# Second products of two FFNs: six of 22 half-pairs by seven quarter products

## The chip, the cores and the metric

One core of one Trainium2 chip runs the whole program. The metric is the device time of one execution in microseconds (us), the median of several runs. The engines are named as in the profile: PE (TensorE, matmuls) with its weight loads PEld, DVE (VectorE), ACT (ScalarE), POOL (GpSimd) and SP (SyncE), whose queue issues the loads. Each engine works through its own instructions in order; they wait for each other by semaphores.

## The reference, cut to what matters

One decoder layer on 512 tokens of width 1024 in float32: an FFN, a token mixer, and a second FFN, each between norms and added to `x`.

```python
def swiglu_ffn(x, w_in, w_out):
    gate, up = jnp.split(x @ w_in, 2, axis=-1)
    return (jax.nn.silu(gate) * up) @ w_out
...
    x = x + 0.5 * rms_norm(swiglu_ffn(rms_norm(x, norm_pre[l, 0]), ffn1_w_in[l], ffn1_w_out[l]), norm_post[l, 0])
    mixed = token_mixer(rms_norm(x, norm_pre[l, 1]), ...)
    x = x + rms_norm(mixed, norm_post[l, 1])
    x = x + 0.5 * rms_norm(swiglu_ffn(rms_norm(x, norm_pre[l, 2]), ffn2_w_in[l], ffn2_w_out[l]), norm_post[l, 2])
```

`ffn1_w_out` and `ffn2_w_out` are 2816 x 1024. The change is in the products `(...) @ w_out`, called the second products here: 512 tokens, 2816 hidden channels, 1024 columns.

## The kernel before, in words

**Number format.** A float32 operand is split into two parts that the matmul takes: `hi`, a rounded copy made by ACT, and `lo`, the rest, made by DVE. A product is three matmuls, hi hi, hi lo and lo hi (`mm3`, lines 125 to 129). Making the two parts is called a conversion here: one ACT cast and one DVE subtraction, of 128 x 1024 elements for a weight tile (`split`, lines 209 and 211) as for a hidden tile (`h_tile`, lines 672 and 673).

**Weights.** `weights` (line 136) turns a list of items, in the order of use, into loads with due places. Loads go out on SP's queue into rings of raw buffers (`raw`, 3 deep, and `raw2`, 5 deep; the second products use `raw2`). `split` converts the next item into one of four slots of one large tile `w`; `feed` does so while fewer than four slots are taken, `pull` hands a slot to the matmuls, `drop` gives it back. A slot can begin 16 elements earlier (`late`).

**First products** (`ffn_in`, `prod`, `after`). They already use seven products instead of eight on quarter matrices; their matmuls have 256 columns (line 489). Their left operands lie in the four tiles `xq` and in three tiles with the tag `s`; POOL adds raw weights for them (line 223). Their result, the hidden rows `hf`, is 22 rows of 128 channels x 512 tokens.

**Second products** (`ffn_out`, line 676). Two adjacent rows of `hf` are a pair (`PAIRS` is 11). The 1024 output columns are taken in two halves of 512. For each half, for each of the 11 pairs, the kernel converts the pair's hidden tile (`h_tile`, three buffers with the tag `s`; the last one goes to `xq[3]`), pulls the weight tile of 2 x 128 rows by 512 columns, and runs, for each of four chunks of 128 tokens, 2 x 3 matmuls of 512 columns into that chunk's accumulator, a bank of PSUM. One pair in one half is a half-pair: 24 matmuls; there are 22 in each FFN. After the first half-pair the last first product (`p4` of the last group) is run. PSUM has eight banks, handed out by `ps`; the four accumulators of a half take four.

**The end of a stage.** The first half's accumulators are squared and multiplied by the norm's gain (`post0`). The last four half-pairs of the second half are held back: their four weights are pulled together, and then the chunks are finished one after the other (`mm`, called by `last`, line 406): chunk 0 with all four weights, then chunk 1, 2 and 3. After each chunk come the post-norm and the addition to `x` (`post1`), and, in the first FFN, the next norm (`norm`). The transposes of the normed rows on PE (`trans`) stand after chunk 2 for chunk 0 and inside chunk 3 for chunk 1. In the second FFN the rows are stored and there is nothing to transpose.

**What sets the order.** Here the order is not written out by hand (only the program's start is). The code is traced from top to bottom; a planner then lets each engine take, of what is ready at its place in a planned time line, what was traced first, and writes this order down for good. Buffers of one tag are handed out as they come free.

Of the kernel before, what the change touches and what calls it, by code (L numbers as in the profile page):

```python
# [14 lines left out]
P = 128  # L15
# [43 lines left out]
class Item:  # L59

    def __init__(self, key, loads, rows=None, adds=(), dst=None):
        self.key, self.loads, self.rows, self.adds, self.dst = key, loads, rows, adds, dst
        self.reads = {key, *(k for pair in adds for k in pair)}


class Layer:
# [117 lines left out]
    def split(self):  # L186
# [5 lines left out]
        if it.dst:  # L192
            w = it.dst()
        else:
            if self.wt is None:
                self.wt = self.wp.tile([P, 2 * D * WBUF + PAD], F32R, name="w")

            taken = {(n, late) for n, late, _ in self.slot.values()}
            fit = [(n, late) for late in (True, False) for n in self.free if (n - 1 if late else n + 1, not late) not in taken]
            n, late = next(f for f in fit if not f[1] or (it.key[0] == "mix" and b == 512))  # L200
# [453 lines left out]
    def ffn_in(self):  # L654
# [8 lines left out]
        self.feed()  # L663
        self.lag()

    def h_tile(self, k2, dst=None):

        t = dst
        if t is None:
            t = self.place(self.hpool.tile([P, 2 * D + PAD], F32R, tag="s", bufs=3, name=self.name("hs")), 2)  # L670
        src = self.hf[:, 2 * k2 : 2 * k2 + 2, :]
        self.nc.scalar.copy(t[:, 0], src)
        self.nc.vector.tensor_tensor(t[:, 1], src, t[:, 0].bitcast(F32), op=ALU.subtract)  # L673
        return t

    def ffn_out(self, gpost_row, scale, after, trans, head):
        NK2, LAST = PAIRS, 4
        seq = [k2 for _ in range(2) for k2 in range(NK2)]
        hs = self.hs
        made = [len(hs)]  # L680

        def more(n):
            while made[0] < min(n, len(seq)):
                k2 = seq[made[0]]
                last = made[0] == len(seq) - 1
                dst = self.xq[3].rearrange("p b k t -> p b (k t)").rearrange("p b (k t) -> p b k t", k=2) if last else None
                hs.append(self.h_tile(k2, dst))
                made[0] += 1

        def out_mm(ps, w, h, k2, i):  # L690
            for kk in range(2):
                k = 2 * k2 + kk
                s = slice(i * P, (i + 1) * P)
                self.mm3(ps, h[:, 0, kk, s], h[:, 1, kk, s], w[:, 0, kk, :], w[:, 1, kk, :], k == 0, k == NF - 1)

        g = self.gain("gpost", gpost_row)
        ys = []
        n = 0
        for half in range(2):
            acc = [self.ps() for _ in range(NT)]  # L700
            for k2 in range(NK2 - LAST if half else NK2):
                more(n + 2)
                w = self.pull()
                more(n + 3)
                h = hs.popleft()
                for i in range(NT):
                    out_mm(acc[i], w, h, k2, i)
# [9 lines left out]
        for k2 in range(NK2 - LAST, NK2):  # L717
# [12 lines left out]


# [73 lines left out]
    def ffn_items(self, name, w_in, w_out):  # L805
# [29 lines left out]
            dst = (lambda n=stay[p]: self.stay[n]) if p in stay else None  # L835
            made.append(Item((name, t, place[p]), own.get((p, t), ()), None, adds.get((p, t), ()), dst))
        for h in range(2):
            for k2 in range(PAIRS):
                src = w_out[k2 * 2 * P : (k2 + 1) * 2 * P, h * 512 : (h + 1) * 512].rearrange("(k p) d -> p k d", p=P)
                key = (name, "out", h, k2)  # L840
                made.append(Item(key, [Load(key, src, 2, 512, "raw2", 5, 8)]))
                if h == k2 == 0:
                    made.append(Item((name, PAIRS - 1, "a"), ()))
        return made

    def small_params(self):

# [711 lines left out]
```

## Time and profile before

| | us |
|---|---|
| median of 3 runs | 937.13 |
| lowest, highest | 936.61, 937.19 |
| profiled execution, device time | 936.74 |
| its span in the trace | 935.0 |
| PE busy | 926.7 |
| DVE busy | 700.1 |
| ACT busy | 468.7 |
| second products of the first FFN in the span, about | 226 to 350 |
| second products of the second FFN, about | 806 to 929 |

All durations in the prediction are from the profiled execution. Times in the trace count from the span's start. A group row shows line, engine, operation, output <- inputs, shapes and count, then busy time, the mean duration of one in ns, and the idle time of the engine before such instructions with what ended it. A row of the order in time begins with start and duration in us. A matmul's duration reaches past the start of the next one, so that what matmuls cost is read from their starts.

### The profile page before, as it was taken

What the parts mean: (1) busy time and instruction counts of PE and PEld (TensorE: products, weight loads), DVE (VectorE), ACT (ScalarE), POOL (GpSimd) and SP (SyncE); (2) the same over time, 40 slices, a digit from 0 to 9 for tenths busy, and PEclk for the clock granted to TensorE, in tenths of its full rate; (3) what the DMA queues carried; (4) which work ended last, traced back from release to release, by engine and by line L of the source; (5) the groups of instructions that cost most, each with busy time, mean ns of one, the idle gap of its engine ahead of it and who ended that gap; (6) DMA issues with size and microseconds to landing.
All of it is one profiled execution on the core that took longest, in us unless ns stands there. A gap on an engine that the chain in (4) does not pass through costs nothing.

```text
span 935.0 us, 16820 instructions
## 1 busy us (share of the span) xinstructions
PE 926.7 (99%) x7021; PEld 850.6 (91%) x7021; DVE 700.1 (75%) x785; ACT 468.7 (50%) x639; POOL 289.9 (31%) x225
## 2 busy tenths in 40 slices
PE   9999999999999999999999999999999999999997
PEld 7999999999888889998888888999999999988885
DVE  6798999998545466688766655887999999844543
ACT  7645445455334345987654254853444454534431
POOL 3535555661000027000020301445455655100001
PEclk9999999999999999999999999999999999999999
DMA  9243334425323005422423135213333422332202
GB/s 318 89 136 114 113 97 131 128 99 158 113 91 106 7 3 126 108 83 70 136 70 113 46 108 185 90 46 113 114 111 117 134 91 91 116 110 91 91 0 91
DMA packets 81992, 97.10 MB, mean 104 GB/s; under 512 B 4178, under 2 KB 61558, under 8 KB 81915
## 3 DMA queue, kind: packets, MB, share of 16 engines
q1 hardware_dynamic: 81306, 94.44, 32.4%
q8 instruction: 55, 0.90, 0.4%
q0 software_dynamic: 320, 1.06, 0.3%
q10 hardware_dynamic: 288, 0.52, 0.2%
q14 instruction: 23, 0.18, 0.1%
HBM read 93.90 MB, written 2.11 MB: 103 GB/s over the span
## 4 chain that ended last, share of the span: by engine, by line
PE 97%; DVE 1%; POOL 1%; issue 1%; ACT 1%; DVEq 0%; POOLq 0%; ACTq 0%
PE ps L489 46%; PE ps L127 13%; PE ps L129 13%; PE ps L128 13%; PE ps L434 6%; PE ps L268 1%; PE ps L1058 1%; POOL col L355 0%; PE ps L1328 0%; PE ps L1131 0%; PE ps L1296 0%; PE ps L116 0%; ACT junk L354 0%; PE ps L123 0%; PE ps L1097 0%
## 5 line engine op out<-in xcount | busy, mean ns | idle before, releaser
L211 DVE TENSOR_TENSOR w<-raw,w 128x1024 fp32r<-128x1024 f32 x214 | 364.2, 1710 | 129.5 <-ACT w L209 129.5
L209 ACT CAST w<-raw 128x1024 fp32r<-128x1024 f32 x214 | 223.9, 1052 | 305.6 <-PE ps L129 104.5
L223 POOL TENSOR_TENSOR raw<-raw,raw 128x1024 f32<-128x1024 f32 x80 | 221.0, 2763 | 171.8 <-DVE w L211 161.3
L489 PE MATMUL ps<-xq,w 128*128 128x256 f32 x2016 | 238.1, 277 | 0.0
L489 PEld LDWEIGHTS ps<-xq,w 128*128 128x128 f32 x2016 | 233.7, 188 | 0.2
L489 PE MATMUL ps<-sq,w 128*128 128x256 f32 x1440 | 171.0, 277 | 0.0
L489 PEld LDWEIGHTS ps<-sq,w 128*128 128x128 f32 x1440 | 167.4, 188 | 0.0
L129 PE MATMUL ps<-w,hs 128*128 128x512 f32 x336 | 131.0, 390 | 0.0
L127 PE MATMUL ps<-w,hs 128*128 128x512 f32 x336 | 130.9, 390 | 0.0
L128 PE MATMUL ps<-w,hs 128*128 128x512 f32 x336 | 130.8, 389 | 0.0
L127 PE MATMUL ps<-w,xq 128*128 128x512 f32 x208 | 83.2, 400 | 0.1
L128 PE MATMUL ps<-w,xq 128*128 128x512 f32 x208 | 81.0, 390 | 0.0
L129 PE MATMUL ps<-w,xq 128*128 128x512 f32 x208 | 81.0, 391 | 0.0
L129 PEld LDWEIGHTS ps<-w,hs 128*128 128x128 f32 x336 | 63.1, 188 | 13.8 <-DVE hs L673 0.7
L127 PEld LDWEIGHTS ps<-w,hs 128*128 128x128 f32 x336 | 63.1, 188 | 13.0
L128 PEld LDWEIGHTS ps<-w,hs 128*128 128x128 f32 x336 | 63.1, 188 | 12.8
L355 POOL TENSOR_SCALAR col<-col 128x1 f32<-128x1 f32 x24 | 10.5, 437 | 198.8 <-ACT junk L354 198.6
L434 PE MATMUL ps<-xq,w 128*128 128x256 f32 x480 | 55.8, 278 | 0.0
L434 PEld LDWEIGHTS ps<-xq,w 128*128 128x128 f32 x480 | 55.4, 188 | 0.2 <-issue 0.2
L673 DVE TENSOR_TENSOR hs<-hf,hs 128x1024 fp32r<-128x1024 f32 x42 | 51.1, 1217 | 0.0
L355 POOL TENSOR_SCALAR col<-col,col 128x1 f32<-128x1 f32 x24 | 10.0, 418 | 119.5 <-ACT junk L354 119.2
L129 PEld LDWEIGHTS ps<-w,xq 128*128 128x128 f32 x208 | 39.0, 188 | 8.8 <-DVE xq L275 0.3
(233 smaller groups left out, 939.5 us busy)
## 6 DMA issues: line engine op xcount, KB each, us to landing
raw<-in_ffn_w_in_dram SPq DMA_DIRECT2D x88, 512.0 KB, 4.4
raw<-in_ffn_w_out_dram SPq DMA_DIRECT2D x44, 512.0 KB, 3.9
raw<-in_w_mix_in_dram SPq DMA_DIRECT2D x28, 512.0 KB, 3.8
raw<-in_w_mix_out_dram SPq DMA_DIRECT2D x8, 512.0 KB, 3.7
out_dram<-xs SPq DMA_DIRECT2D x8, 256.0 KB, 2.1
xs<-in_x_dram SPq DMA_DIRECT2D x6, 256.0 KB, 6.2
gpost<-in_norm_post_dram SPq DMA_DIRECT2D x3, 512.0 KB
gpre<-in_norm_pre_dram SPq DMA_DIRECT2D x2, 512.0 KB, 4.1
```

The costliest lines, as they stand in the source:

```text
L127: mm(ps, sh, mh, start=start, stop=False, **kw)
L128: mm(ps, sh, ml, start=False, stop=False, **kw)
L129: mm(ps, sl, mh, start=False, stop=stop, **kw)
L209: nc.scalar.copy(hi, raw)
L211: nc.vector.tensor_tensor(lo, raw, hi.bitcast(F32), op=ALU.subtract)
L223: nc.gpsimd.tensor_tensor(o, o, c, op=ALU.add)
L268: self.nc.tensor.transpose(pt[:, c * P : (c + 1) * P], src[:, k * P : (k + 1) * P], self.ident)
L355: nc.gpsimd.tensor_scalar(m, ss, s2 / D, b, op0=ALU.mult, op1=ALU.add)
L434: mm(ps[:, u0:u1], w[:, a, k, :], self.xop(k, b, u0, u1), start=k + n + m == 0, stop=k == ND - 1 and n == 2, skip_group_check=True,)
L489: self.nc.tensor.matmul(ps[:, c], wb[b][:, k, v], left[d][:, k, :], start=first and a + n + k == 0, stop=n == 2 and k == KH - 1, skip_grou ...
L673: self.nc.vector.tensor_tensor(t[:, 1], src, t[:, 0].bitcast(F32), op=ALU.subtract)
L1058: nc.tensor.matmul(sc[r, o : o + u.stop - u.start], k8[:, m, r], q8[:, m, u], start=True, stop=True, skip_group_check=True)
```

## The change

Of the 11 pairs, three (3, 4 and 2) are computed in both halves by seven quarter products instead of eight: six of 22 half-pairs. For one such half-pair the hidden tile is a 2 x 2 matrix of quarters (two rows of `hf` by two halves of the tokens), and the weight tile is a 2 x 2 matrix too (two rows by two halves of the 512 columns). Products 1 to 7 each multiply a quarter or a sum of quarters, 128 channels by 256 tokens with 128 channels by 256 columns: two chunks of tokens, three matmuls of 256 columns each.

- **Order.** `OUT` lists both halves: `p` is a plain half-pair, `k` and `s` go by seven products, `r` is plain with a hidden tile that the first half left over. The four last half-pairs of the second half are plain.
- **Sums of weights.** After the first conversion of a weight tile of `k` or `s`, DVE forms four differences in place in the raw tile (`w_sums`, each 128 x 256); the raw tile is then converted a second time into another slot. So such a half-pair pulls two slots.
- **Sums of hidden quarters.** `s_tile` forms four sums (DVE, 128 x 256 each), in place in `hf` or, for pair 2 in the first half, in two extra tiles, and converts them. Pairs 3 and 4 keep both converted tiles in the four `xq` tiles for the second half; pairs 9 and 10, last in the first half, are first in the second, with the tiles still there.
- **Banks.** Products 2, 3 and 4 go straight into the accumulators. Products 1, 5, 6 and 7 go into four further banks, each with both chunks, and are summed there over the half's three such pairs.
- **Gather.** After the last of the three, one ACT copy and four DVE additions form four terms in SBUF, in `hf` rows no longer needed. One plain half-pair is run; then, ahead of each chunk's matmuls of the next plain half-pair, DVE adds that chunk's term to its accumulator.
- **Ends.** Chunks 0 and 1 run through the last four weights together: weight 0 for both, weight 1 for both, and so on.
- **Places.** `h_tile` begins 112 elements later in its buffer; weight slots of the second products may begin 32 elements earlier.

```diff
+OUT = ("p0 p1 p5 k3 k4 p6 s2 p7 p8 p10 p9".split(), "r9 r10 k3 k4 s2 p0 p1 p5 p6 p7 p8".split())
...
+            taken = {n: late for n, late, _ in self.slot.values()}
+            want = 0 if b != 512 else 1 if it.key[0] == "mix" else 2
+            fits = lambda n, late: taken.get(n - 1, 2) >= late >= taken.get(n + 1, 0)
+            n, late = next((n, late) for late in (*range(want, -1, -1), 1, 2) for n in self.free if fits(n, late))
...
+        if it.then:
+            it.then(raw)
...
+                if kind == "k" and h == 0:
+                    kept[k2] = self.h_tile(k2, homes.popleft()), self.s_tile(k2, homes.popleft())
+                elif kind == "s":
+                    kept[k2] = self.h_tile(k2), self.s_tile(k2, None, h == 0)
+                elif kind == "p":
+                    kept[k2] = self.h_tile(k2, flat(self.xq[3]) if made[0] == len(seq) - 1 else None), None
+                hs.append(kept[k2])
...
+        def seven(acc, sums, begun, w, wt, h, hs_, stop):
+            tok = lambda q, t: slice(HALF * q + P * t, HALF * q + P * (t + 1))
+            col = lambda q: slice(HALF * q, HALF * (q + 1))
+            for p, a, ka, qa, b, kb, qb in (
+                (1, h, 0, 0, w, 0, 0), (5, hs_, 1, 1, wt, 0, 0), (6, hs_, 0, 0, wt, 1, 1), (7, hs_, 0, 1, wt, 0, 1),
+                (2, h, 1, 0, w, 1, 0), (3, hs_, 1, 0, w, 1, 1), (4, h, 1, 1, wt, 1, 0),
+            ):
+                fresh = p in sums and p not in begun
+                begun.add(p)
+                for t in range(2):
+                    if p in sums:
+                        out = sums[p][:, col(t)]
+                    else:
+                        out = acc[2 * (p == 4) + t][:, col(p == 3)]
+                    for m, (x, y) in enumerate(((0, 0), (0, 1), (1, 0))):
+                        self.nc.tensor.matmul(
+                            out, a[:, x, ka, tok(qa, t)], b[:, y, kb, col(qb)],
+                            start=fresh and t + m == 0, stop=stop and m == 2, skip_group_check=True,
+                        )
+
+        def gather(sums, pairs):
+            x, y = (self.hf[:, 2 * k : 2 * k + 2, :].rearrange("p t (c v) -> p t c v", c=2) for k in pairs)
+            u = self.sp.tile([P, D], F32, tag="xn", bufs=1, name=self.name("u2"))[:, :512]
+            two = lambda t: t.rearrange("p (t v) -> p t v", t=2)
+            self.nc.scalar.copy(x[:, :, 0], two(sums[1]))
+            add(two(u), two(sums[6]), x[:, :, 0])
+            add(x[:, :, 1], two(sums[5]), two(u))
+            add(y[:, :, 0], two(sums[7]), two(u))
+            add(y[:, :, 1], two(sums[5]), y[:, :, 0])
+            return [t[:, i].rearrange("p c v -> p (c v)") for t in (x, y) for i in range(2)]
...
+                if kind in "pr":
+                    since += terms is not None
+                    for i in range(NT):
+                        if since == 2:
+                            add(acc[i], acc[i], terms[i])
+                        out_mm(acc[i], w, h, i, m == 0, since == 1 or m == PAIRS - 1)
+                else:
+                    seven(acc, sums, begun, w, wt, h, hs_, k2 == fast[-1])
+                    self.drop(wt)
                 self.drop(w)
+                if fast and k2 == fast[-1]:
+                    terms = gather(sums, [k for _, k, kind in self.outs(0) if kind == "k"])
...
-            for m, (k2, w) in enumerate(ws):
-                out_mm(acc[i], w, hs[m], k2, i)
+            for m, (k2, w) in enumerate(ws if i != 1 else ()):
+                for j in (0, 1) if i == 0 else (i,):
+                    out_mm(acc[j], w, hs[m][0], j, False, m == LAST - 1)
...
+                made.append(Item(key, [Load(key, src, 2, 512, "raw2", 5, 8)], then=self.w_sums if kind in "ks" else None))
+                if kind in "ks":
+                    made.append(Item(key, ()))
...
+    def w_sums(self, raw):
+        sub = lambda out, a, b: self.nc.vector.tensor_tensor(out, a, b, op=ALU.subtract)
+        (b11, b12), (b21, b22) = ((raw[:, k, :HALF], raw[:, k, HALF:]) for k in range(2))
+        sub(b11, b12, b11)
+        sub(b12, b22, b12)
+        sub(b22, b22, b11)
+        sub(b21, b21, b22)
+
+    def s_tile(self, k2, dst=None, whole=False):
+        tt = lambda out, a, b, op: self.nc.vector.tensor_tensor(out, a, b, op=op)
+        rows = [self.hf[:, 2 * k2 + k, :] for k in range(2)]
+        sums = [self.st("sum") for _ in range(2)] if whole else rows
+        (a11, a21), (a12, a22), (s2, s3), (s4, s1) = ((t[:, :HALF], t[:, HALF:]) for t in rows + sums)
+        tt(s1, a22, a21, ALU.add)
+        tt(s3, a11, a21, ALU.subtract)
+        tt(s2, s1, a11, ALU.subtract)
+        tt(s4, a12, s2, ALU.subtract)
+        if not whole:
+            return self.h_tile(k2, dst)
+        t = self.h_place()
+        for k, src in enumerate(sums):
+            self.nc.scalar.copy(t[:, 0, k], src)
+            self.nc.vector.tensor_tensor(t[:, 1, k], src, t[:, 0, k].bitcast(F32), op=ALU.subtract)
+        return t
```

More of the change, by code (lines that the diff above doesn't have):

```diff
@@ L59, with __init__ @@
 class Item:
-    def __init__(self, key, loads, rows=None, adds=(), dst=None):
-        self.key, self.loads, self.rows, self.adds, self.dst = key, loads, rows, adds, dst
+    def __init__(self, key, loads, rows=None, adds=(), dst=None, then=None):
+        self.key, self.loads, self.rows, self.adds, self.dst, self.then = key, loads, rows, adds, dst, then
         self.reads = {key, *(k for pair in adds for k in pair)}
@@ L664, in ffn_in, with h_place @@
         self.lag()
+    def h_place(self):
+        return self.place(self.hpool.tile([P, 2 * D + PAD], F32R, tag="s", bufs=3, name=self.name("hs")), 2, True)
     def h_tile(self, k2, dst=None):
-        t = dst
-        if t is None:
-            t = self.place(self.hpool.tile([P, 2 * D + PAD], F32R, tag="s", bufs=3, name=self.name("hs")), 2)
+        t = self.h_place() if dst is None else dst
         src = self.hf[:, 2 * k2 : 2 * k2 + 2, :]
@@ L676, in ffn_out @@
     def ffn_out(self, gpost_row, scale, after, trans, head):
[L677 to L678 removed]
+        LAST = 4
+        seq = [(h, k2, kind) for h in range(2) for _, k2, kind in self.outs(h)]
         hs = self.hs
+        for _ in range(len(hs)):
+            hs.append((hs.popleft(), None))
         made = [len(hs)]
+        flat = lambda q: q.rearrange("p b k t -> p b (k t)").rearrange("p b (k t) -> p b k t", k=2)
+        kept, homes = {}, deque(flat(q) for q in self.xq)
@@ L682, in more @@
         def more(n):
             while made[0] < min(n, len(seq)):
[L684 to L687, printed above, removed]
+                h, k2, kind = seq[made[0]]
+                if kind == "k" and h == 0:
[4 more added lines that the diff above has]
+                    kept[k2] = self.h_tile(k2, flat(self.xq[3]) if made[0] == len(seq) - 1 else None), None
@@ L696, in ffn_out @@
+        add = lambda out, a, b: self.nc.vector.tensor_tensor(out, a, b, op=ALU.add)
         g = self.gain("gpost", gpost_row)
@@ L716, in ffn_out @@
         ws = []
-        for k2 in range(NK2 - LAST, NK2):
+        for k2 in range(PAIRS - LAST, PAIRS):
             ws.append((k2, self.pull()))
```

27 lines of the change are left out of this document (14 added, 13 removed).

## The prediction

> **What bounds the kernel now.** I read the page first (busy shares, slices, the chain that ended last), then the windows of the stage that the change touches, then the groups and the order in time inside it.
>
> ```profile
> PE 926.7 (99%) x7021; PEld 850.6 (91%) x7021; DVE 700.1 (75%) x785; ACT 468.7 (50%) x639; POOL 289.9 (31%) x225
> PE   9999999999999999999999999999999999999997
> DVE  6798999998545466688766655887999999844543
> ...
> PE 97%; DVE 1%; POOL 1%; issue 1%; ACT 1%; DVEq 0%; POOLq 0%; ACTq 0%
> ```
>
> PE is busy in every slice and holds 97% of the chain. So a microsecond of matmuls taken away is a microsecond won, as long as nothing else becomes late. DVE is the engine to watch: nearly full in the first products, half full in the second ones (slices 11 to 14 and 36 to 40). The second products of both FFNs, seen in two stretches well inside them (columns: length, busy time of PE, weight loads, DVE, ACT, POOL, clock, DMA):
>
> ```profile
> 236.00:325.00 89.00, 89.00 (x394) 73.68 (x394) 42.30 (x39) 35.66 (x41) 1.39 (x4) 1.00 0.23 78
> 816.00:905.00 89.00, 89.00 (x394) 73.68 (x394) 42.75 (x39) 35.73 (x42) 1.39 (x4) 1.00 0.25 80
> ```
>
> PE has no gap, DVE works 42.3 of 89 us, ACT 35.7, POOL 1.4, the DMA engines a quarter. The reader is to see the spare half of DVE and ACT: the change spends there to save on PE.
>
> **What a half-pair costs on PE.** The page's matmul durations (277 ns for 256 columns, 390 for 512) overlap, so the price is the distance between starts.
>
> ```profile
> 317.89 0.39 PE L127 MATMUL ps<-w,hs 128*128 128x512 f32 x1
> ...
> 328.77 0.39 PE L127 MATMUL ps<-w,hs 128*128 128x512 f32 x1
> ```
>
> Between these starts lie 48 matmuls: (328.77 - 317.89) / 48 = 0.2267 us each, and a half-pair of 24 costs 5.44 us. For 256 columns there are two prices, one from the chain (the second FFN's first products) and one from the lone product p4, which stands between matmuls of 512 columns:
>
> ```profile
> 603.04 202.85 PE ps L489 x1776
> ```
>
> ```profile
> 811.18 2.99 PE L489 MATMUL ps<-xq,w 128*128 128x256 f32 x24
> 814.01 0.39 PE L127 MATMUL ps<-w,hs 128*128 128x512 f32 x1
> ```
>
> The long run gives 202.85 / 1776 = 0.1142 us each; p4 gives (814.01 - 811.18) / 24 = 0.118. A half-pair by seven quarter products has 7 x 2 x 3 = 42 matmuls of 256 columns instead of 24 of 512: 4.80 us at the first price, 4.95 at the second. The sevens stand between matmuls of 512 columns as p4 does, so I take 4.95. **Twelve of them save 12 x (5.44 - 4.95) = 5.9 us**; at the other price 7.7.
>
> A page of the Trainium skill speaks against this: "TensorE: Matmul & The Clock Gate", section Back-to-back issue gap, gives a sustained spacing of about 81 ns at 128 columns and 131 ns at 512, so that a matmul's price grows far slower than its columns. By that rule, with an estimate of 98 ns at 256 columns (a third of the way from 128 to 512), 42 would cost 4.1 us against 24 x 131 = 3.1, and the change would lose about 11.5 us. The starts above, 0.2267 against 0.114 to 0.118, do not agree with it.
>
> **What DVE and ACT pay.** Prices by distances between starts:
>
> ```profile
> 225.32 0.67 DVE L508 TENSOR_TENSOR hf<-q,ps 128x512 f32<-128x512 f32 x1
> 225.92 0.68 DVE L508 TENSOR_TENSOR ps<-q,ps 128x512 f32<-128x512 f32 x1
> ```
>
> ```profile
> 272.94 1.23 DVE L211 TENSOR_TENSOR w<-raw,w 128x1024 fp32r<-128x1024 f32 x1 [3.08 <-ACT w L209]
> 274.08 1.22 DVE L673 TENSOR_TENSOR hs<-hf,hs 128x1024 fp32r<-128x1024 f32 x1
> 278.37 1.22 DVE L211 TENSOR_TENSOR w<-raw,w 128x1024 fp32r<-128x1024 f32 x1 [3.08 <-ACT w L209]
> ```
>
> ```profile
> L1350 DVE TENSOR_TENSOR y<-ps,col 128x256 f32<-128x256 f32 x8 | 3.0, 420 | 6.6 <-POOL col L1347 6.6
> ```
>
> ```profile
> 230.94 1.05 ACT L209 CAST w<-raw 128x1024 fp32r<-128x1024 f32 x1 [4.82 <-PE ps L129]
> 231.90 1.04 ACT L672 CAST hs<-hf 128x1024 fp32r<-128x1024 f32 x1
> ```
>
> A conversion takes 1.14 us of DVE (274.08 - 272.94) and 0.96 of ACT (231.90 - 230.94); an operation on 512 columns 0.60 of DVE. For 256 columns the row shows 0.42; less the same 0.08 that a following operation gains elsewhere it is 0.34 (bounds 0.34 and 0.42). The rows 272.94 to 278.37 are today's rhythm: two conversions, then 3.08 us of idle DVE, every 5.44 us.
>
> Per FFN the change adds six conversions of second weights (6.8 us of DVE), forty sums on 256 columns (24 of weights, 16 of hidden parts: 13.6), two gathers of four additions and eight additions into the accumulators (16 x 0.60 = 9.6), two half conversions (1.2), and takes one conversion away (22 become 21, since the parts of pairs 3 and 4 and the tiles of 9 and 10 are used twice). That is 30 us more of DVE; ACT gets five whole casts and four half ones, 7 us. Over the 120 us of the stage DVE goes from about 50 to 80 us. This lies beside PE as long as no stretch runs over. The work is not tied to its place in the code either:
>
> ```profile
> 237.84 1.23 DVE L673 TENSOR_TENSOR xq<-hf,xq 128x1024 fp32r<-128x1024 f32 x1 [1.11 <-ACT xq L672]
> ```
>
> The only conversion into xq belongs to the last half-pair of the stage and is read over 90 us later (the row at 331.95 below); it ran as soon as DVE was free. So an engine takes what is ready, the earlier traced first, and the parts of pairs 3 and 4 will be made in the first 20 us. But a thing traced late goes behind everything traced before it that is ready too.
>
> The loads stay 22 of 512 KB per FFN, in the new order on SP's queue, into the same five buffers:
>
> ```profile
> raw<-in_ffn_w_out_dram SPq DMA_DIRECT2D x44, 512.0 KB, 3.9
> ```
>
> A seven keeps its buffer until the second conversion, about one half-pair longer; the load five places on still has more than 10 us where it needs 3.9. That costs nothing while DMA is a quarter busy; without that cover it would be one landing, 3.9 us.
>
> **Place one: the additions after the last seven.** In each half the sums of products 1, 5, 6 and 7 go into the accumulators between the next two half-pairs; PE cannot start the second of these before the first addition is through. Let E be the end of seven s2 in the first half. DVE has first the conversions of p7's tile and p8's weights (slots free at E - 4.95; casts 0.96 each, so ready from E - 3.9, through by E - 1.6), then the gather (4 x 0.60, to E + 0.8). Then four conversions traced before the additions, two of weights and two of tiles, whose slots s2 has just given back: to E + 0.8 + 4 x 1.14 = E + 5.36. The first addition ends at E + 5.96. PE has 5.44 us of p7: a wait of 0.5. Behind the matmul that waits stand all later ones, so the whole wait is lost. The other additions (0.60 each against 1.36 us of matmuls) then keep ahead. The second half has the same four conversions after s2, and 0.5 as well. **Four waits, 2.0 us.** Bounds: nothing, if a gap in the casts lets additions slip in; and 1.65 each, if the gather ends 0.4 later and the next two conversions get between the second and third addition (0.9 + 0.75).
>
> **Place two: the second weights.** A seven holds two of the four weight slots, so three half-pairs of lead shrink to one. The tightest is s2 in the second half: its slots come free with k3, and the chain cast, conversion, four sums, cast, conversion is 0.96 + 1.14 + 1.36 + 0.96 + 1.14, with four hand-overs of 0.04 (the cast at 230.94 lasts 1.05, DVE started at 232.03) 5.7 us. Cover: k4 (4.95) and product 1 (0.71), which needs only the first weight: 5.66. I take 0; bounds 0 and 0.5.
>
> **Place three: the first two chunks together.** In the first FFN the normed rows of chunk 0 are transposed after chunk 2.
>
> ```profile
> 331.95 0.39 PE L129 MATMUL ps<-w,xq 128*128 128x512 f32 x1
> ...
> 342.66 1.03 PE L268 MATMUL ps<-ident,xn 128*128 128x128 f32 x8
> ```
>
> ```profile
> 337.65 1.43 DVE L373 SCALAR_TENSOR_TENSOR xn<-xs,col,gpre 128x512 f32<-128x512 f32 x2 [2.06 <-POOL col L359]
> ```
>
> Chunk 0 ended at 332.34 and its rows were ready at 339.08, 6.7 us later, 3.6 before PE came to them. Now chunk 0 ends 1.36 us before chunk 1, and only 1.36 + 5.44 = 6.8 us before that place, and chunk 1's chain runs on the same engines. I take 0.3, once; bounds 0 and 1.0. In return the third and fourth weights of the last group are needed at 5.4 and 8.2 us instead of 2.7 and 4.1: no wait was there, so nothing is gained. In the second FFN nobody transposes: 0. The stage's last two chunks and the end of the kernel stay as they are.
>
> **Placement.** The hidden tiles move by 112 elements and the second weights by up to 32. That placement can matter shows in two groups with the same work:
>
> ```profile
> L489 PE MATMUL ps<-xq,w 128*128 128x256 f32 x954 | 112.4, 277 | 0.0
> ...
> L489 PE MATMUL ps<-xq,sq 128*128 128x256 f32 x96 | 11.9, 282 | 0.0
> ```
>
> ```profile
> L129 PE MATMUL ps<-w,hs 128*128 128x512 f32 x336 | 131.0, 390 | 0.0
> ...
> L129 PE MATMUL ps<-w,xq 128*128 128x512 f32 x208 | 81.0, 391 | 0.0
> ```
>
> 5 ns on each of the 768 wide matmuls that stay would be 3.8 us; I take 0 (bounds -1 and +3.8), since the wide ones show one duration, 390 and 391, for tiles in two places.
>
> **The sum.** -5.9 + 2.0 + 0.3 = -3.6. The profiled execution took 936.74 us (span 935.0 and 1.74 around it): 933.1. The median of the runs is 937.13, 0.39 above it, so **933.5**.
>
> **The rivals.** *The narrow price is the long run's, 0.1142, and the waits are short*: -7.7 + 1 = 930.4. For it: the long runs of narrow matmuls have it; against it: p4 does not, and a faster seven leaves DVE less time before the additions. Chance 0.16.
>
> *The additions eat the gain*: four waits near 1.65 us, -5.9 + 6.6 + 0.3 = +1.0, or half of that; 935.3 to 938.1, no change. For it: the order of tracing. Against: an idle moment of DVE is enough to let an addition in. Chance 0.18.
>
> *Slower: DVE runs over in the same place.* From k3's start to the first addition DVE must do about 20.6 us (eleven conversions 12.5, s2's own parts and sums 5.1, gather and addition 3.0) in 25.7. If the gather ends 1.1 us later than I time it, the four conversions end at E + 6.5, when the two next (cast by p7's end + 1.0) are ready and go ahead: the first addition ends at E + 9.4, a wait of 4 us. In two of four places: -5.9 + 8 + 1 + 0.3 = +3.4, 940.5; in all four 947. For it: DVE conversions took 1.71 on the average of the whole kernel,
>
> ```profile
> L211 DVE TENSOR_TENSOR w<-raw,w 128x1024 fp32r<-128x1024 f32 x214 | 364.2, 1710 | 129.5 <-ACT w L209 129.5
> ```
>
> and three such in the stretch would do it. Against: here they take 1.23, with POOL at rest (1.39 of 89 us). Chance 0.13.
>
> *The change does not save PE time*: if a narrow matmul cost more than 5.44 / 42 = 0.1295 us. From the overlapping durations, 42 x 277 against 24 x 390 ns, +2.3 us each, +27 us, 964. The starts speak against it. The spacing of the Trainium skill, above, would be this case. Chance 0.01.
>
> **Numbers.** My forecast, 931.0 to 935.2, has 0.52. Faster by over 0.2% (1.87 us; about what a measurement of this kernel can tell from no change) is my case and the first rival: 0.68. Same 0.18, slower 0.14. The range: below 929.8 only both prices at their best lead, above 938.2 the slower rival; I leave out about 0.15.
>
> **What would show it.** 504 matmuls of 256 columns from the second products, 0.118 apart, 4.95 us a seven; 226 weight conversions instead of 214; DVE busy about 760 us. Gaps of PE of about 0.5 us before the second half-pair after each s2, released by a DVE addition into the accumulator, and none inside a seven. If the sevens are 4.8 us, or gaps stand inside them or exceed 1.5 us, I am wrong there; if the wide matmuls are no longer 0.2267 apart, the placement is the cause.

## The result, and the profile after

The changed kernel takes **959.91 us** (median; 959.26 to 960.69) against 937.07 beside it: ratio **1.0245** (95% interval 1.0230 to 1.0260). That is 22.8 us slower, and 26 above the forecast of 933.5. The profiled execution took 960.48, its span is 958.8.

From the page of the changed kernel, the lines that answer to those of before; the third is the chain that ended last, of which PE now holds 53%, not 97%:

```profile
PE 933.1 (97%) x7237; PEld 859.6 (90%) x7237; DVE 763.8 (80%) x911; ACT 482.2 (50%) x657; POOL 287.2 (30%) x225
...
PEclk9999999999999899999999999999999999999999
...
PE 53%; DVE 7%; issue 2%; ACT 1%; POOL 0%; DVEq 0%; POOLq 0%; ACTq 0%
...
L128 PE MATMUL ps<-w,hs 128*128 128x512 f32 x240 | 96.7, 404 | 10.3 <-DVE ps L739 10.3
```

DVE's work is as forecast (763.8 us busy, about 760 forecast; 226 conversions). What is new is PE standing idle. Lines have moved: the wide matmuls are L128 to L130 (L127 to L129 before), the narrow ones of the sevens L723, the head of the next stage L448 (L444); L213 is the weight conversion (L211), L678 the hidden tiles' (L673), L739 all additions, of the gather and into the accumulators. PE's waits (us in all, times, longest):

```profile
PE ps L128 <- DVE ps L739: 10.3, 4, 4.2
PE ps L723 <- DVE w L213: 3.2, 5, 0.9
PE ps L448 <- DVE w L213: 1.8, 2, 1.0
```

**The additions** cost 10.3 us instead of 2.0: 0.94 in the first half and 4.23 in the second, in both FFNs. The waits are not all: in PE's timeline behind the long one each matmul starts 0.427 us after the one ahead of it (327.60, 328.03 and so on), for 13 matmuls:

```profile
326.61 0.76 PE L128 MATMUL ps<-w,hs 128*128 128x512 f32 x1 [4.23 <-DVE ps L739]
...
327.60 0.63 PE L130 MATMUL ps<-w,hs 128*128 128x512 f32 x1
328.03 0.63 PE L128 MATMUL ps<-w,hs 128*128 128x512 f32 x1
...
332.94 0.39 PE L128 MATMUL ps<-w,hs 128*128 128x512 f32 x1
```

The windows give the clock there (the third number from the end): 0.50 behind the pause, then 0.99.

```profile
326.60:332.60 6.00, 5.99 (x14) 4.74 (x15) 1.66 (x3) 0.00 (x0) 0.00 (x0) 0.50 0.00 0
332.60:338.20 5.60, 5.60 (x25) 4.48 (x25) 1.88 (x2) 2.00 (x2) 0.00 (x0) 0.99 0.00 0
```

Against 0.2333 apart, the pace of the others (below), this costs 3.0 us in the first FFN and 1.8 in the second, where 8 matmuls are slow; 0.24 of each is the restart of PE, which the two short waits pay as well. The Trainium skill has this in "TensorE: Matmul & The Clock Gate", section What's actually happening: after an idle window of some 3.4 us the array runs at half its clock, and its section Wait — 56ns, not 53.3ns? gives 426.7 ns a matmul of 512 columns for that state. The 0.427 agrees; for how long a pause has to be, see the experiments.

**The pace** of matmuls changed everywhere in the stage. Wide ones, 48 matmuls between two rows, and the sevens, 84 in one row:

```profile
280.56 0.39 PE L128 MATMUL ps<-w,hs 128*128 128x512 f32 x1
...
291.76 0.39 PE L128 MATMUL ps<-w,hs 128*128 128x512 f32 x1
```

```profile
301.56 9.69 PE L723 MATMUL ps<-w,xq 128*128 128x256 f32 x84
311.08 1.74 PE L723 MATMUL ps<-w,hs 128*128 128x256 f32 x12
313.11 3.68 PE L723 MATMUL ps<-w,hs 128*128 128x256 f32 x30 [0.29 <-DVE w L213]
```

(291.76 - 280.56) / 48 = 0.2333 us instead of 0.2267; (311.08 - 301.56) / 84 = 0.1133 instead of the 0.118 forecast. **The end of the first FFN**, from its last wide matmul to the mixer's first long run, takes 377.22 - 360.49 = 16.7 us; the kernel before took 13.6.

```profile
360.49 1.08 PE L448 MATMUL ps<-xq,w 128*128 128x256 f32 x8
...
377.22 2.99 PE L438 MATMUL ps<-xq,w 128*128 128x256 f32 x24
```

```profile
349.92 3.25 PE L444 MATMUL ps<-xq,w 128*128 128x256 f32 x24
...
363.53 2.66 PE L434 MATMUL ps<-xq,w 128*128 128x256 f32 x22
```

### The profile page after: what moved, and what is told of

The parts are those of the page before. It is cut to its first block, busy times and chain, and to the rows that moved or that the text cites. A ratio compares the mean times of both kernels' runs of the same rounds, so it can differ in the third digit from the quotient of the medians.

```text
span 958.8 us, 17403 instructions
## 1 busy us (share of the span) xinstructions
PE 933.1 (97%) x7237; PEld 859.6 (90%) x7237; DVE 763.8 (80%) x911; ACT 482.2 (50%) x657; POOL 287.2 (30%) x225
## 4 chain that ended last, share of the span: by engine, by line
PE 53%; DVE 7%; issue 2%; ACT 1%; POOL 0%; DVEq 0%; POOLq 0%; ACTq 0%
PE ps L493 19%; PE ps L128 7%; PE ps L130 7%; PE ps L129 7%; PE ps L438 6%; DVE w L213 2%; PE ps L723 1%; DVE hs L678 1%; PE ps L1150 1%; PE ps L448 1%; ACT w L211 1%; PE ps L272 1%; DVE raw L913 0%; DVE xq L678 0%; DVE hf L922 0%
## 5 line engine op out<-in xcount | busy, mean ns | idle before, releaser
L213 DVE TENSOR_TENSOR w<-raw,w 128x1024 fp32r<-128x1024 f32 x226 | 375.7, 1672 | 77.9 <-ACT w L211 77.1
L211 ACT CAST w<-raw 128x1024 fp32r<-128x1024 f32 x226 | 235.2, 1051 | 284.8 <-POOL raw L225 88.3
L128 PE MATMUL ps<-w,hs 128*128 128x512 f32 x240 | 96.7, 404 | 10.3 <-DVE ps L739 10.3
L129 PE MATMUL ps<-w,hs 128*128 128x512 f32 x240 | 96.5, 402 | 0.0
L130 PE MATMUL ps<-w,hs 128*128 128x512 f32 x240 | 96.3, 401 | 0.0
L128 PE MATMUL ps<-w,xq 128*128 128x512 f32 x208 | 83.3, 401 | 0.1
L130 PE MATMUL ps<-w,xq 128*128 128x512 f32 x208 | 81.1, 391 | 0.0
L129 PE MATMUL ps<-w,xq 128*128 128x512 f32 x208 | 81.0, 390 | 0.0
L359 POOL TENSOR_SCALAR col<-col 128x1 f32<-128x1 f32 x24 | 7.2, 298 | 200.9 <-ACT junk L358 200.8
L128 PEld LDWEIGHTS ps<-w,hs 128*128 128x128 f32 x240 | 46.1, 192 | 22.7 <-issue 12.0
L130 PEld LDWEIGHTS ps<-w,hs 128*128 128x128 f32 x240 | 46.2, 193 | 11.0
L129 PEld LDWEIGHTS ps<-w,hs 128*128 128x128 f32 x240 | 46.1, 192 | 10.4
L130 PEld LDWEIGHTS ps<-w,xq 128*128 128x128 f32 x208 | 39.0, 188 | 8.8 <-DVE xq L279 0.3
L128 PEld LDWEIGHTS ps<-w,xq 128*128 128x128 f32 x208 | 39.1, 188 | 8.7 <-ACT xq L278 0.7
```

Source lines behind the costliest of these rows:

```text
L128: mm(ps, sh, mh, start=start, stop=False, **kw)
L129: mm(ps, sh, ml, start=False, stop=False, **kw)
L130: mm(ps, sl, mh, start=False, stop=stop, **kw)
L211: nc.scalar.copy(hi, raw)
L213: nc.vector.tensor_tensor(lo, raw, hi.bitcast(F32), op=ALU.subtract)
L359: nc.gpsimd.tensor_scalar(m, ss, s2 / D, b, op0=ALU.mult, op1=ALU.add)
```

## The experiments

Ratios are to the kernel before, with 95% intervals.

**1. The places alone, on the kernel before.**

```diff
-            n, late = next(f for f in fit if not f[1] or (it.key[0] == "mix" and b == 512))
+            want = 0 if b != 512 else 1 if it.key[0] == "mix" else 2
...
-            t = self.place(self.hpool.tile([P, 2 * D + PAD], F32R, tag="s", bufs=3, name=self.name("hs")), 2)
+            t = self.place(self.hpool.tile([P, 2 * D + PAD], F32R, tag="s", bufs=3, name=self.name("hs")), 2, True)
```

> The kernel before, with only the new places: hidden tiles moved by 112 elements, weights of the second products by 32. In the changed kernel the wide matmuls stand 0.2333 us apart, before 0.2267. Theory 'places': the places alone make it; some 1,050 wide matmuls times 0.0066 us, +7 us, 944. Rival 'company': the wide ones are slower because narrow ones and pauses stand between them; then they stay 0.2267 apart here and the time stays 937.

946.34 us, 1.0094 (1.0079 to 1.0109); its four runs lie from 944.55 to 947.00, and the profile is that of the fastest. From its timeline, 48 matmuls apart:

```profile
275.98 0.39 PE L127 MATMUL ps<-w,hs 128*128 128x512 f32 x1
...
287.18 0.39 PE L127 MATMUL ps<-w,hs 128*128 128x512 f32 x1
```

11.20 / 48 = 0.2333: the places alone make it, with no seven and no pause near. Another 2.1 us came at the end of the first FFN (15.7 us; see 4).

**2. The changed kernel with the old places.**

```diff
-            want = 0 if b != 512 else 1 if it.key[0] == "mix" else 2
+            want = int(b == 512 and it.key[0] == "mix")
...
-        return self.place(self.hpool.tile([P, 2 * D + PAD], F32R, tag="s", bufs=3, name=self.name("hs")), 2, True)
+        return self.place(self.hpool.tile([P, 2 * D + PAD], F32R, tag="s", bufs=3, name=self.name("hs")), 2)
```

> The changed kernel with the places of before. Theory 'places': the 768 wide matmuls go back to 0.2267 apart, -5.1 us, and the 504 narrow ones from 0.1135 to the 0.118 of the lone p4, +2.3: 957. Rival 'company': wide ones stay at 0.2333, 960.

957.90, 1.0217 (1.0201 to 1.0232).

```profile
280.40 0.39 PE L128 MATMUL ps<-w,hs 128*128 128x512 f32 x1
...
291.28 0.39 PE L128 MATMUL ps<-w,hs 128*128 128x512 f32 x1
```

```profile
300.80 10.05 PE L723 MATMUL ps<-w,xq 128*128 128x256 f32 x84
310.69 1.47 PE L723 MATMUL ps<-w,hs 128*128 128x256 f32 x11
```

Wide 0.2267 again, narrow 9.89 / 84 = 0.1177. So between these two kernels the new places buy 4.4 ns on each of 504 narrow matmuls (2.2 us) and pay 6.6 ns on each of the wide ones. (For the narrow ones the place is not the whole cause: see 10 to 12.)

**3. The additions one half-pair later.**

```diff
                     for i in range(NT):
-                        if since == 2:
-                            add(acc[i], acc[i], terms[i])
-                        out_mm(acc[i], w, h, i, m == 0, since == 1 or m == PAIRS - 1)
+                        out_mm(acc[i], w, h, i, m == 0, since == 2 or m == PAIRS - 1)
+                    if since == 2:
+                        for i in range(NT):
+                            add(acc[i], acc[i], terms[i])
```

> The changed kernel with the additions into the accumulators one half-pair later in both halves (behind the second half-pair after the last seven, no longer before it). Theory 'order': the waits of 0.9 and 4.2 us per FFN (10.3 in all) go, and with them the slower clock behind the long ones (84 matmuls at 0.269 and 0.254 instead of 0.2333 apart, 4.8 us): about 945. Rival 'too much work': DVE has no room in this stretch, so the conversions are late instead and gaps of the same sum come elsewhere: 955 to 960.

943.85, 1.0074 (1.0059 to 1.0089): 16.1 us of the 22.8 back. PE waits for no addition any more, the other waits stay (the largest is that of the sevens for their weights, 3.2 us in five waits, as before), and the 84 matmuls behind the place stand 0.2333 apart. "Too much work" is out: nothing else became late by more than 0.2 us.

**4. The last group's chunks one after another.**

```diff
-            for m, (k2, w) in enumerate(ws if i != 1 else ()):
-                for j in (0, 1) if i == 0 else (i,):
-                    out_mm(acc[j], w, hs[m][0], j, False, m == LAST - 1)
+            for m, (k2, w) in enumerate(ws):
+                out_mm(acc[i], w, hs[m][0], i, False, m == LAST - 1)
```

> The changed kernel with the last group's chunks ending one after another again. From the end of the first FFN's second products to the mixer's first long run the changed kernel takes 16.7 us, the one before 13.6. Theory 'pair': two chunks that end together send their norms one behind the other through ACT, POOL and DVE, and the second one's transposes are late; undone, the 3.1 us come back: 957. Rival 'backlog': the end is late because the stage before it is; then 960. Third: the last group's third and fourth weights, due 2.7 and 4.1 us sooner, are late now: over 960.

958.03, 1.0225 (1.0208 to 1.0242). The end took 373.85 - 358.13 = 15.7 us: one microsecond back, not three. PE now did three of the eight transposes, then stood for 1.8:

```profile
358.13 1.08 PE L448 MATMUL ps<-xq,w 128*128 128x256 f32 x8
359.06 0.49 PE L272 MATMUL ps<-ident,xn 128*128 128x128 f32 x3
361.37 2.10 PE L448 MATMUL ps<-xq,w 128*128 128x256 f32 x16 [1.82 <-DVE w L213]
...
373.85 3.34 PE L438 MATMUL ps<-xq,w 128*128 128x256 f32 x28
```

**5. Places, pair and additions undone: only the sevens stay.**

> The changed kernel with the additions one half-pair later, the places of before and the last group's chunks one after another: only the sevens and their preparation are left. With pair or places alone undone, the end of the first FFN took 16.6 and 15.7 us against 13.6 of the kernel before. Theory 'either is enough': the end is late as long as one of the two is there, and comes back whole with both undone; then 937.1 - 12 x (5.44 - 4.95) + about 3.5 us of gaps inside the sevens = 934.7. Rival 'one each': the parts add, and 0.5 to 1 us of the end stays late: 935.5.

937.52, 1.0003 (0.9994 to 1.0012), 2.8 us above the one, 2.0 above the other. The end is whole again (363.30 - 349.66 = 13.6 us), so "one each" is out:

```profile
349.66 3.26 PE L448 MATMUL ps<-xq,w 128*128 128x256 f32 x24
...
363.30 13.88 PE L438 MATMUL ps<-xq,w 128*128 128x256 f32 x121
```

What is missing is in the sevens: five waits, 3.1 us in all, inside them, and the matmuls beside each wait are slower too. The twelve sevens gained only what they lost there.

**6. The additions sooner, not later.**

```diff
-                        if since == 2:
-                            add(acc[i], acc[i], terms[i])
                         out_mm(acc[i], w, h, i, m == 0, since == 1 or m == PAIRS - 1)
+                    if since == 1:
+                        for i in range(NT):
+                            add(acc[i], acc[i], terms[i])
```

> The changed kernel, the additions traced directly behind the first half-pair after the last seven, so ahead of the two conversions (a second part of weights and one of a hidden tile) that follow in the trace; PE needs them as early as in the changed kernel. Theory 'order': these two conversions, 2.3 us, are what the additions stand behind: the long waits shrink from 4.2 to about 1.8 us, twice 2.4, and 1 to 4 us of slower clock go with them: 950 to 954. Rival 'DVE is full': additions come no sooner, or the conversions are now late by as much: 958 to 960.

951.48, 1.0149 (1.0134 to 1.0163), inside the range of "order". DVE's timeline at the same place in the changed kernel and here:

```profile
315.24 0.68 DVE L739 TENSOR_TENSOR u<-ps,hf 128x512 f32<-128x512 f32 x1
315.84 1.21 DVE L678 TENSOR_TENSOR xq<-hf,xq 128x1024 fp32r<-128x1024 f32 x1
316.97 0.68 DVE L739 TENSOR_TENSOR hf<-ps,u 128x512 f32<-128x512 f32 x1
317.57 1.21 DVE L678 TENSOR_TENSOR hs<-hf,hs 128x1024 fp32r<-128x1024 f32 x1
318.71 0.68 DVE L739 TENSOR_TENSOR hf<-ps,u 128x512 f32<-128x512 f32 x1
319.31 1.21 DVE L213 TENSOR_TENSOR w<-raw,w 128x1024 fp32r<-128x1024 f32 x1
320.44 0.68 DVE L739 TENSOR_TENSOR hf<-ps,hf 128x512 f32<-128x512 f32 x1
321.04 1.21 DVE L213 TENSOR_TENSOR w<-raw,w 128x1024 fp32r<-128x1024 f32 x1
322.18 1.22 DVE L678 TENSOR_TENSOR hs<-hf,hs 128x1024 fp32r<-128x1024 f32 x1
323.50 1.22 DVE L213 TENSOR_TENSOR w<-raw,w 128x1024 fp32r<-128x1024 f32 x1
324.64 1.22 DVE L678 TENSOR_TENSOR hs<-hf,hs 128x1024 fp32r<-128x1024 f32 x1
325.78 2.48 DVE L739 TENSOR_TENSOR ps<-ps,hf 128x512 f32<-128x512 f32 x4
```

```profile
322.26 1.22 DVE L678 TENSOR_TENSOR hs<-hf,hs 128x1024 fp32r<-128x1024 f32 x1
323.39 2.48 DVE L739 TENSOR_TENSOR ps<-ps,hf 128x512 f32<-128x512 f32 x4
```

Read the first from the top: the gather's four additions (L739 into u and hf) take turns with five conversions, then come two more, 323.50 and 324.64, and only then the additions PE waits for. In the second fence these stand ahead of the two: they start 2.4 us sooner, PE waits 1.76, and no matmul behind it is slow (clock 1.00 in the 5.7 us that follow).

**7 and 8. Matmuls in the pause** (18, then 6, behind the first half-pair after the last seven, in the second half).

```diff
+                    if half and since == 1:
+                        for _ in range(18):
+                            self.nc.tensor.matmul(sums[5], h[:, 0, 0, :P], w[:, 0, 0, :], start=True, stop=True)
```

> The changed kernel with 18 more wide matmuls (their result is not used) where PE waits 4.2 us in the second half of each FFN. They take 18 x 0.2333 = 4.2 us, so the wait is filled and not shortened. Theory 'clock': the pause makes the clock fall (0.79 and 0.87 in the windows behind it) and the matmuls behind stand 0.254 to 0.269 apart; filled, they stand 0.2333 apart, and 4.8 us come back: 955. Rival: the matmuls behind the pause are slow for another reason (operands late, accumulators just written): 960 to 961.

> The changed kernel with 6 instead of 18 more wide matmuls in the long pauses (their result is not used), so that PE pauses 4.23 - 1.40 = 2.8 us instead of 4.2 (with 18: none; with the additions sooner: 1.76, and the matmuls behind it were not slow). If a pause of 2.8 us makes the clock fall as one of 4.2 does, 8 to 13 matmuls behind it stand 0.427 apart and the time stays near 960; if not, the 4 to 5 us of slow matmuls go and it is about 955.

954.95 (1.0190; 1.0176 to 1.0204) and 950.41 (1.0137; 1.0118 to 1.0155). The first gave the expected time, but not in the expected way, and the second shows it: there was no pause of 2.8 us left, only 0.35. With the extra matmuls in the program the planner gave DVE another order, with the first two additions (with 18: all four) ahead of the two conversions. So these two show once more what the order is worth; of the clock they show only that without a long pause no matmul is slow.

**9. The sevens apart** (on top of 5).

```diff
-OUT = ("p0 p1 p5 k3 k4 p6 s2 p7 p8 p10 p9".split(), "r9 r10 k3 k4 s2 p0 p1 p5 p6 p7 p8".split())
+OUT = ("p0 p1 p5 p6 k3 p7 k4 p8 s2 p10 p9".split(), "r9 r10 k3 k4 s2 p0 p1 p5 p6 p7 p8".split())
```

> As the one with three parts undone, and in the first half the sevens stand apart: pair 6 ahead of the first, 7 and 8 between them. In the changed kernel DVE is full in the 20 us ahead of the first two (9.97 of 10 us busy), and PE waits 0.9 us (first FFN) and 1.7 (second) inside them for the second part of weights. Theory 'DVE is full there': with half-pairs between them these waits go, 2.6 us and about 1 us of slower matmuls behind them less than the kernel with three undone: 931 to 932. Rival 'chain': the second weights are late because their chain of cast, sums and conversion is longer than one half-pair wherever the seven stands: no gain, 934 to 935.

**932.67, 0.9952 (0.9939 to 0.9965): faster than both kernels**, though 0.7 us above the 931 to 932 expected. The first two sevens now run without a wait, 4.95 us each as forecast; of the waits only s2's in the second half are left:

```profile
PE ps L723 <- DVE w L213: 0.5, 2, 0.3
```

"Chain" is out. That two sevens in a row are by themselves too much is out as well: in the second half of the changed kernel k3 and k4 follow each other without a wait (the row of 84 at 301.56), with no parts of hidden tiles to make.

**10 to 12. Which place** (each on top of 9): only the weights moved, only the hidden tiles, both.

> The spread kernel (932.7) with only the weights of the second products moved by 32 elements. Theory 'difference': the pace goes by the difference of the two operands' addresses, which is 256 bytes (modulo 512) for hidden tiles in the kernel before (0.2267 us apart), 192 with both moved (0.2333) and 128 here; then the 600 wide matmuls at 128 stand 0.2333 apart, +4 us. Rival 'hidden tiles': it is the hidden tiles' own place; then they stay 0.2267 apart. In both the end of the first FFN takes 15.7 us instead of 13.6, if the new weight slots are what made it late: 939 or 935.

> The spread kernel (932.7) with only the hidden tiles moved by 112 elements; difference 320. Theory 'difference': not 256, so the 720 wide matmuls stand 0.2333 apart, +4.8: 937.5. Rival 'weights': their place decides; 0.2267 apart, 932.7. In both the end of the first FFN takes 13.6 us as in the kernel before, since the weight slots are the old ones.

> The spread kernel (932.7) with both new places, weights by 32 and hidden tiles by 112 elements. The wide matmuls go to 0.2333 apart as with the places alone in the kernel before (+4 to 5 us), the narrow ones to 0.1134 (-2). Theory 'both moved': the end of the first FFN takes 15.7 us as in the two runs with both moved and no chunk pair, +2.1: 937 to 938. Rival 'another order': those two were late for their own order of the engines; here it takes 13.5: 935 to 936.

The difference is that of the addresses of the weights and a hidden tile (of the tag `s`) in the built program, in bytes modulo 512, for most wide matmuls; the paces are by distances of starts, over long rows.

| moved | us | ratio (interval) | difference | wide, us apart | narrow | end of first FFN |
|---|---|---|---|---|---|---|
| none (9) | 932.67 | 0.9952 (0.9939 to 0.9965) | 256 | 0.2267 | 0.1177 to 0.1198 | 13.6 |
| weights | 935.49 | 0.9981 (0.9971 to 0.9990) | 128 | 0.2320 to 0.2333 | 0.1135 to 0.1202 | 13.4 |
| hidden tiles | 931.92 | 0.9940 (0.9925 to 0.9956) | 320 | 0.2289 | 0.1133 | 13.5 |
| both | 935.22 | 0.9980 (0.9971 to 0.9989) | 192 | 0.2333 | 0.1133 to 0.1177 | 13.6 |

The row of hidden tiles, from its timeline, (287.17 - 276.18) / 48 and (306.99 - 297.47) / 84:

```profile
276.18 0.39 PE L128 MATMUL ps<-w,hs 128*128 128x512 f32 x1
...
287.17 0.39 PE L128 MATMUL ps<-w,hs 128*128 128x512 f32 x1
...
297.47 9.68 PE L723 MATMUL ps<-w,xq 128*128 128x256 f32 x84
306.99 1.74 PE L723 MATMUL ps<-w,hs 128*128 128x256 f32 x12
```

For the wide ones neither place decides alone: each of them moves the pace, as "difference" says, but not to one value for all that is not 256. Its size (0.2333) was wrong for the hidden tiles alone. In the mixer of the kernel before, tiles at other addresses with the same difference of 256 stand 0.2267 apart too, (467.36 - 461.01) / 28.

For the narrow ones the difference does not decide. In the kernel with both moved the same 84 matmuls, k3 and k4 in the second half, have the same addresses in both FFNs (a difference of 192), and take 307.47 - 297.95 = 9.52 us in the first and 887.49 - 877.60 = 9.89 in the second, 0.1133 and 0.1177 each:

```profile
297.95 9.69 PE L723 MATMUL ps<-w,xq 128*128 128x256 f32 x84
...
877.60 10.06 PE L723 MATMUL ps<-w,xq 128*128 128x256 f32 x84
```

And with only the hidden tiles moved these 84, whose own tiles lie in `xq` and did not move, went from 0.1177 (9) to 0.1133. What else sets the pace of the narrow ones stays open.

The kernel with the hidden tiles moved has the narrow ones' gain at a third of the wide ones' loss and is the fastest measured here, though its interval overlaps that of 9. The end of the first FFN is 13.4 to 13.6 in all, with any places: "both moved" is out, and the 15.7 of 1 and 4 belong to an order of engines of their own.

**13 and 14. How long a pause** (on top of 6; the diff is that of 13, and 14 has a third term in the list; the maximum of a term with itself leaves it as it is).

```diff
+                    if half and since == 1:
+                        for i in (0, 1):
+                            self.nc.vector.tensor_tensor(terms[i], terms[i], terms[i], op=ALU.max)
```

> The kernel with the additions sooner (951.5, pause of 1.76 us in the second half of each FFN), with two DVE operations on 512 columns (a maximum of a term with itself, 0.6 us each) ahead of these additions: a pause of about 3.0 us. Theory 'whole window': the clock falls only when PE rests longer than some 3.4 us; then no slow matmuls behind it, 951.5 + 2.4 = 954. Rival 'shorter': matmuls at 0.427 apart behind this pause, 2 to 3 us more in each FFN: 958 to 960.

> The same with three such operations: a pause of about 3.6 us. Theory 'whole window': as the pause is hardly longer than 3.4 us, the clock falls seldom; if it falls only beyond 3.4, this run may show it in one FFN and not in the other. Without it 955; with it in both 960.

955.67 (1.0202; 1.0185 to 1.0219) and 957.66 (1.0220; 1.0205 to 1.0235). The pauses were 2.83 and 2.84 us in the two FFNs of the one, and 3.43 and 3.56 in those of the other. Behind all four the clock fell, for 6 to 8 matmuls:

```profile
322.60:325.50 2.90, 0.08 (x1) 0.02 (x1) 2.90 (x5) 1.99 (x2) 0.00 (x0) 0.91 0.01 3
325.50:328.60 3.10, 3.09 (x8) 2.49 (x9) 3.10 (x5) 0.00 (x0) 0.00 (x0) 0.53 0.00 0
```

"Whole window" is out: 2.83 us of rest are enough here, 1.76 are not.

## Why the prediction was wrong, step by step

The 23.8 us between the two spans, by the traces (us):

| term | forecast | measured |
|---|---|---|
| twelve sevens at the pace of their long runs | -5.9 | -8.3 |
| waits inside sevens, and slower matmuls beside them | 0 | +5.9 |
| waits for the additions | +2.0 | +10.3 |
| half clock behind the long ones, restart included | not in the sum | +4.8 |
| wide matmuls, pace and other restarts | 0 | +5.0 |
| end of the first FFN, its transposes' waits with it | +0.3 | +4.2 |
| p4 | 0 | -0.2 |
| start of the first second products, mixer, last microseconds | 0 | +2.0 |

Rounding leaves 0.1. Why the last row came is not followed up; 0.9 of it lies between the mixer's first long run and the second FFN's second products (443.1 us instead of 442.2). The first two: twelve half-pairs of 5.46 (the whole stage of before, its first and last ones in it) against 12 x 4.77, and the sevens together took 63.1 instead of 57.2. Every sign came that the prediction had named as showing it wrong: sevens near 4.8 us, gaps inside them, gaps above 1.5 us, and wide matmuls no longer 0.2267 apart.

- **Bound and bookkeeping were right**: a microsecond of PE is a microsecond; narrow matmuls pipeline, so the rival by the Trainium skill's spacing ("TensorE: Matmul & The Clock Gate", section Back-to-back issue gap: 131 ns at 512 columns; 227 to 233 here) is out; DVE's sum and the count of conversions came out.
- **Place one is the step that failed**, and most of the loss. It said that the second half has "the same four conversions after s2, and 0.5 as well". There are five: the one into xq (315.84), which the prediction itself named as belonging to the last half-pair of the stage, is made there. The conversions are through at 323.32, 6.7 us after s2's end at 316.63, where the forecast had 5.36; the rival "DVE runs over in the same place" named 6.5 as the point from which two more go ahead, an end of the first addition at 9.4 and a wait of 4 us. That order and those times came (9.8 and 4.23), in two of the four places; the other two waited 0.94 where 0.5 was said. The mechanism was in the text; it got a chance of 0.13, though the 1.1 us of slack that it asked for is less than a single conversion, 1.14. Experiments 3 and 6 show that the order makes the wait. That the fifth conversion tipped it is read from the timeline; no run moved it alone. And the order is the planner's, not the chip's choice: at 323.32 the additions had all that they needed (their terms since 321.12, their accumulators since 322.4), while the first of the two conversions still waited for its cast (322.42 + 1.04 = 323.46).
- **A wait was priced at its own length.** The rival's 8 us of long waits were 8.5, and 4.8 of half clock (0.5 of it restart) came on top. The trace of before has no pause in this stage and could not show this. The page of the Trainium skill that the prediction cites for its spacing has the rule (above), and it belonged into the price of this rival.
- **Placement: 0 was taken, bounds -1 and +3.8**; it was +5.0 on the wide and -2.2 on the narrow (experiments 1, 2 and 10 to 12). The reason given, one duration of 390 and 391 ns for tiles in two places, read the wrong column: durations overlap. The starts of before had the signal. The last chunks' matmuls on the tile in `xq` stood up to 0.2333 apart (six from 330.78 to 332.18), the long rows on the other hidden tiles 0.2267.
- **Place two**: 0 to 0.5 was said for s2 in the second half, and 0.29 it was, in each FFN. But k3 and k4 in the first half, where DVE makes the hidden tiles' parts too, waited 0.85 to 0.88 three times. The prediction summed DVE over the stage and over the 25.7 us from k3's start to the first addition, not over the first 20 us, where DVE (the third busy time of the row) has no room:

```profile
230.00:240.00 10.00, 10.00 (x57) 8.68 (x57) 9.97 (x16) 3.05 (x3) 0.00 (x0) 1.00 0.34 108
```

- **Place three**: 0.3 against about 4. The pair was the change's, and the end takes 16.5 to 16.7 us in every kernel here whose two chunks end together, 13.4 to 13.6 in those without, 1 and 4 excepted. On DVE the second chunk's norm and all that follows stand behind the first one's, and the weights' second part for the next stage behind them (begun at 365.26; PE waited 1.0 us for it, and 0.8 for the next). Why 1 and 4 took 15.7 without the pair stays open: PE's transposes are cut into three and five there; what made the planner do so was not tried.

## What to carry to other kernels

Where an engine's order is fixed ahead by a planner, the question is not whether it has room but what stands ahead of the one instruction that PE needs; list these one by one, and if the slack is less than one of them, price the case that one more comes. Work that ends a long overlap (a gather, an addition into an accumulator) is best given a whole step more, which cost nothing here and brought 16 us. Read a matmul's price from the distance of starts, for each tile's place and each stage apart.

## What the runs showed of the hardware

- **A pause of PE costs more than itself.** Behind 0.94 and 1.76 us no matmul is at half clock, and 0.24 us go to the restart. Behind all ten pauses of 2.83 to 4.23 us (two each in the changed kernel, 2, 4, 13 and 14) stand 6 to 13 matmuls of 512 columns at about 0.427 us, and the loss beyond the pause itself is 1.6 to 3.0 us. The slow ones need not be the first: in the second FFN of the changed kernel three matmuls behind the pause of 4.23 us still kept their pace (922.30 to 923.08). The Trainium skill's page ("TensorE: Matmul & The Clock Gate", section What's actually happening) puts the fall behind an idle window of about 3.4 us; here the measurement decides, 2.83 was enough.
- **An operand's place, moved by 128 or 448 bytes, changes the pace of wide matmuls by 1 to 3%.** For 512 columns it is 0.2267 us where the two operands' addresses differ by 256 (modulo 512), 0.2289 at 320, 0.2333 at 192, 0.2320 to 0.2333 at 128. For 256 columns it is 0.1133 or 0.1177 (4%), and neither the place nor the difference settles which.
